# A list schedule in which all-SBUF VectorE instructions and GpSimd arithmetic take turns, with transfer leads and slacks set anew

## The chip, the cores and the metric

The kernel runs on one core of a Trainium2 chip. A time is device microseconds of one execution of the whole program. The core has five engines, each with its own queue that it works through in order: PE (matrix products, and transposes as products with an identity), DVE (VectorE), ACT (ScalarE), POOL (GpSimd) and SP, which here only issues transfers. SBUF holds the working tiles, PSUM takes what PE writes.

## The reference

One layer of an encoder serves 2048 prompt frames and 8 running streams of 16 new frames, with shared weights:

```
h = rms_norm(x, norm_g);  z = h @ w_in                       # (T,1024) @ (1024,3584)
u_a, v_a, g_a, q, k, v, g_b = split(z)
y_a = u_a * (tril(W_s) @ rms_norm(v_a) + b_s) * silu(g_a)    # per 128-position chunk, 4 heads
q, k = rms_norm(q), rms_norm(k)                              # two 64-wide halves per head
p1, p2 = softmax(q1 k1' / 8 - alibi), softmax(q2 k2' / 8 - alibi)   # block-causal, or past + new
y_b = rms_norm((p1 - lam * p2) @ v) * (1 - lam_init) * silu(g_b)
out = x + concat(y_a, y_b) @ w_out                           # also returned: new k, v and v_a rows
```

All tensors are float32. Most operands of PE are written as a sum of two rounded parts, high and low, so that one product becomes three (`mm3`) or two.

## The kernel before, in words

The program is first written down in one order and then sorted by a list scheduler, `Order`, once per build. What is written down:

- **Projection** (`stream`, `project`): 17 tiles of 128 frames (16 prompt tiles, one tile with all sample frames). `xload` scales a tile's rows on DVE (L552), `xpose` transposes it on PE (`x_tp`, L367) and `split` makes the high part with ACT (L428) and the low part with DVE (L429). `load_w` loads a block of the weights, makes the high part on ACT (L595) and the low part on DVE (L596). `project` gathers 3 products for each of 8 slices of 128 inputs, so 24 matmuls `acc` per tile and block. `vg_group` follows with squares, `rstd` on POOL (L435, L436), a scaling on DVE (`vn`, L693) and a split (`vhl`).
- **Sample attention** (`sample_scores`, `sample_values`), woven into the projection: cached keys are transposed (`sk_tp`), split into `skT` by ACT and DVE, multiplied (`sS`), completed by POOL (`slo`, L1074) and DVE (L1075); cached values are split by ACT and POOL (`sv`, L429 POOL), then multiplied (`sO`).
- **Prompt attention** (`attention`), in two stages: scores `S`, a running minimum on DVE (L858), exponentials on ACT (L862), the two softmaxes combined by DVE (`ex`, L874) or by ACT and POOL (L877, L878), transposed (`a_tp`), split into `aT`, multiplied with the values (`oT`), normalised (`o_tp`, L925 to L931).
- **Output** (`out_stream`): products `oo` with `w_out`, woven into the second attention stage, the sum with x on POOL (L1279) or DVE (L1281).

`constants` computes lambda from four loaded vectors (`keep1`, L415) by two DVE instructions (L417) near the start.

`Order` then fixes each engine's queue. `depend` finds which instruction needs which. `cost` gives each instruction a duration and a time after which its engine is free. `run` walks through time: the engine that can start earliest takes, of its instructions that are ready, the one that was written down first. An instruction's ready time is its latest producer's end plus a hop per engine plus a slack (L68: 350 ns for PE, 500 ns for SP; L69: `OTHER`, 150 ns for ACT, DVE and POOL). A transfer is taken to need `FETCH` = 3200 ns before its data begin to flow, one transfer after the other. The result is order alone: each engine works through its list, and the semaphores that the tile framework sets between engines stay the same in kind. Nothing on the chip waits for the planned times. In this plan DVE and POOL are independent of each other.

Of the kernel before, what the change touches and what calls it, by code (L numbers as in the profile page):

```python
# [18 lines left out]
PSUM = bass.MemoryType.PSUM  # L19
# [40 lines left out]
class Order:  # L60
# [4 lines left out]
    PE, ACT, DVE, POOL, SP = (mybir.EngineType.PE, mybir.EngineType.Activation, mybir.EngineType.DVE,  # L65
                              mybir.EngineType.Pool, mybir.EngineType.SP)

    SLACK = {PE: 350.0, SP: 500.0}  # L68
    OTHER, FETCH = 150.0, 3200.0  # L69

    class Node:
        def __init__(self, ins, idx):
# [45 lines left out]
    def depend(self):  # L118
        seen, last = {}, {}
        self.uses = {}  # L120
        for n in self.nodes:
            for ap, w in [(a, False) for a in n.reads] + [(a, True) for a in n.writes]:
                t = ap.bass_ap.tensor
                space = str(t.space)
                m, chip = self.region(ap, space), "DRAM" not in space
                lo = ap.bass_ap.offset
                box = lo, lo + sum(s * (k - 1) for s, k in ap.ap) + 1, chip and ap.ap[0][1] < P
                old = seen.setdefault(t.name, [])
                for m2, j, w2, box2 in old:
                    if (w or w2) and j != n.idx and (m & m2 or ((box[2] or box2[2]) and box[0] < box2[1] and  # L130
                                                                box2[0] < box[1])):
                        n.deps.add(j)
                if w and n.engine == self.PE:
                    if t.name in last:
                        n.deps.add(last[t.name])
                    last[t.name] = n.idx
                if w:
                    old[:] = [x for x in old if x[0] & ~m or x[1] == n.idx]
                old.append((m, n.idx, w, box))
                if chip and t.name not in n.tiles:  # L140
                    n.tiles.append(t.name)
                    self.uses.setdefault(t.name, []).append(n.idx)
# [45 lines left out]
    def cost(self, n):  # L188

        kind = type(n.ins).__name__[4:]  # L190
        size = max([math.prod([k for s, k in a.ap[1:]]) for a in n.reads + n.writes] or [1])
        accum = len(n.writes) > 1
        if n.dma:
            return 0.0, 560.0 if n.engine == self.POOL else 400.0
        if n.engine == self.PE:
            size = math.prod([k for s, k in n.writes[0].ap[1:]])
            t = 109.0 if size <= P else 4 + 0.4455 * size
            return t + 165, t
        if n.engine == self.ACT:
            t = 165 + 0.83 * size if kind == "TensorCopy" else 205 + 0.835 * size  # L200
            return (t + 180, t + 90) if accum else (t, t - 105)
        if n.engine == self.DVE:
            t = {"TensorTensor": 160 + 1.04 * size, "TensorReduce": 160 + 1.03 * size, "Memset": 100 + 0.5 * size,
                 "Reciprocal": 162.0}.get(kind, 205 + 1.04 * size)
            if kind == "TensorScalarPtr" and not n.ins.is_scalar_tensor_tensor:
                t = 170 + 0.56 * size
            return (t + 100, t - 40) if accum else (t, t - 85)
        if kind == "Memset":
            return 100 + 0.83 * size, 100 + 0.83 * size
        if "pow" in str(n.ins):  # L210
            return 300 + 200.0 * size, 250 + 200.0 * size
        t = 190 + 2.16 * size if kind == "TensorTensor" else 195 + 1.1 * size
        return t, t - 50

    def run(self):
        N = self.nodes
# [29 lines left out]
        left = {k: len(q) for k, q in self.queue.items()}  # L246
        users = {x: len(self.uses[x]) for x in self.tag}
        last, slot, taken, freed = {}, {}, set(), {}
        free = {n.engine: 0.0 for n in N}
        later, now_, held = {e: [] for e in free}, {e: [] for e in free}, set()  # L250
        out = {e: [] for e in free}
        dma = 0.0

# [18 lines left out]
        def arrive(i):  # L272
            if N[i].new:
                held.add(i)
            else:
                heapq.heappush(later[N[i].engine], (ready[i], i))

        def place():
            for i in sorted(held):
                got = buffer(i)  # L280
                if got:
                    for name, s in got[1]:
                        taken.add(s)
                        slot[name] = s
                        left[s[0]] -= 1
                    ready[i] = max(ready[i], got[0])
                    held.discard(i)
                    heapq.heappush(later[N[i].engine], (ready[i], i))
                    return True
            return False  # L290
# [3 lines left out]
                arrive(n.idx)  # L294
        while place():
            pass
        for _ in N:
            t, _, e = min((free[e] if now_[e] else max(free[e], later[e][0][0]), e.value if hasattr(e, "value") else str(e), e)
                          for e in free if now_[e] or later[e])
            while later[e] and later[e][0][0] <= t:  # L300
                heapq.heappush(now_[e], heapq.heappop(later[e])[1])
            i = heapq.heappop(now_[e])
            n = N[i]
            out[e].append(i)
            if n.dma:
                size = 4 * math.prod([k for s, k in n.writes[0].ap])
                dma = max(t + self.FETCH, dma) + max(size / 280, 60.0)
                end = dma + 200
            else:
                end = t + cost[i][0]  # L310
            free[e] = t + cost[i][1]
            for j in n.after:
                b = N[j].engine
                if b == e and not n.dma and not N[j].dma:
                    r = free[e]
                else:
                    r = end + reach.get(b, 35.0) + (self.SLACK.get(b, self.OTHER) if b != e or n.dma else 0)
                ready[j] = max(ready[j], r)
                N[j].wait -= 1
                if not N[j].wait:  # L320
                    arrive(j)
            more = list(first[i])
            for g in gate[i]:
                g[0] -= 1
                if not g[0]:
                    more += g[2]
            for j in more:
                ready[j] = max(ready[j], t)
                N[j].wait -= 1
                if not N[j].wait:  # L330
                    arrive(j)
            for name in n.tiles:
                if name in users:
                    last[name] = max(last.get(name, 0.0), end + 35)
                    users[name] -= 1
                    if not users[name]:
                        taken.discard(slot[name])
                        freed[slot[name]] = last[name]
            while held and place():
                pass  # L340
# [7 lines left out]
def trunk_step_kernel(  # L348
# [588 lines left out]
    def attention(sb, sl, groups, wmax, nk, nv, nex, comb, eng):  # L937
# [31 lines left out]
        for i, (key, j) in enumerate(units):  # L969
# [33 lines left out]
            for _, run in sorted(events, key=lambda e: e[0]):  # L1003
                yield run()
# [350 lines left out]
```

## Time and profile before

| | |
|---|---|
| median of 3 runs (lowest to highest) | 1421.57 us (1420.43 to 1421.87) |
| the profiled execution: time, span of its instructions | 1421.42 us, 1419.7 us |
| mean granted TensorE clock | 0.993 |
| busy: PE, DVE, ACT, POOL | 1364.3, 904.4, 789.6, 632.8 us |
| read from HBM, written | 130.86 MB, 42.47 MB |

The span runs from the program's first instruction to its last. Where a stretch is named below by two numbers, they are microseconds from the span's start. PE's matmuls overlap in their pipeline, so a busy PE is not PE at its peak; its idle time, and what ended each idle stretch, are listed by the view of waits.

### The profile page before, as it was taken

How to read it: one execution, taken by the hardware profiler on the slowest of the kernel's cores; microseconds unless marked ns; L12 is line 12 of the kernel's file. 1: busy time of each engine (PE TensorE's matmuls, PEld its weight loads, DVE VectorE, ACT ScalarE, POOL GpSimd, SP SyncE). 2: the span in 40 equal slices, each digit the busy share in tenths (PEclk: the TensorE clock that was granted, in tenths of full speed). 3: DMA queues.
4: the chain of work that ended last, by engine and by line, in shares of the span. 5: the costliest groups of instructions: out<-in, count | busy, mean ns of one | idle time of the engine just before them, and what ended most of it. 6: DMA issues, size and time to landing. Idle time of an engine off the chain costs nothing.

```text
span 1419.7 us, 27994 instructions
## 1 busy us (share of the span) xinstructions
PE 1364.3 (96%) x9892; PEld 1264.1 (89%) x9892; DVE 904.4 (64%) x2114; ACT 789.6 (56%) x1778; POOL 632.8 (45%) x796
## 2 busy tenths in 40 slices
PE   5999999999999999999999999998899999999998
PEld 5999999899998889999999999997788888888887
DVE  4432447766665684698987764324788897877722
ACT  4533336766565775566666454224677766676621
POOL 2251544656364564857435142022456545555400
PEclk9999999999999999999999999999899999999999
DMA  6533224554444475635443243245555534432323
GB/s 185 187 89 107 72 75 127 165 152 137 135 128 137 145 211 182 191 98 156 127 110 108 68 130 98 75 131 168 158 149 145 164 102 126 145 103 83 106 82 101
DMA packets 209245, 183.06 MB, mean 129 GB/s; under 512 B 21104, under 2 KB 167024, under 8 KB 209104
## 3 DMA queue, kind: packets, MB, share of 16 engines
q1 hardware_dynamic: 199280, 155.17, 37.0%
q0 software_dynamic: 9824, 26.09, 6.6%
q8 instruction: 78, 1.28, 0.4%
q14 instruction: 63, 0.52, 0.1%
HBM read 130.86 MB, written 42.47 MB: 122 GB/s over the span
## 4 chain that ended last, share of the span: by engine, by line
PE 71%; DVE 10%; ACT 6%; issue 5%; POOL 4%; DMA 3%; SPq 1%; DVEq 0%; POOLq 0%; ACTq 0%
PE acc L363 34%; PE oo L363 11%; PE S L363 7%; PE oT L363 6%; PE a_tp L367 4%; DVE ex L858 2%; DVE ex L874 2%; PE sS L363 2%; ACT ex L862 2%; DVE w L596 1%; PE sk_tp L367 1%; PE sO L363 1%; POOL sv L429 1%; PE y_tp L367 1%; DMA wraw<-in_w_in_dram 1%
## 5 line engine op out<-in xcount | busy, mean ns | idle before, releaser
L363 PE MATMUL acc<-w,xT 128*128 128x256 f32 x5376 | 723.6, 284 | 4.9 <-DVE w L596 2.0
L363 PEld LDWEIGHTS acc<-w,xT 128*128 128x128 f32 x5376 | 678.1, 190 | 17.9 <-DVE w L596 3.8
L363 PE MATMUL oo<-wo,yT 128*128 128x512 f32 x816 | 235.1, 402 | 1.5 <-ACT yT L428 1.2
L363 PE MATMUL S<-kT,qT 128*128 128x512 f32 (+3 forms) x688 | 186.0, 363 | 5.3 <-DVE sst L858 4.1
L862 ACT ACTIVATE ex<-ex,sst 128x128 f32<-128x128 f32 (+15 forms) x128 | 153.8, 1203 | 42.7 <-DVE sst L858 42.2
L596 DVE SCALAR_TENSOR_TENSOR w<-wraw,normg,w 128x256 fp32r<-128x256 f32 x224 | 120.1, 564 | 80.2 <-ACT w L595 73.3
L363 PEld LDWEIGHTS oo<-wo,yT 128*128 128x128 f32 x816 | 146.4, 188 | 26.9 <-ACT yT L428 2.0
L363 PE MATMUL oT<-aT,v 128*128 128x256 f32 x864 | 154.9, 295 | 0.0
L429 POOL TENSOR_TENSOR sv<-svraw,sv 128x512 fp32r<-128x512 f32 (+1 forms) x72 | 98.7, 1375 | 95.8 <-ACT sv L428 74.4
L858 DVE CUSTOM_DVE_ANT_0 ex<-S,dist,sst 128x512 f32<-128x512 f32 (+2 forms) x192 | 123.1, 652 | 27.4 <-PE S L363 25.5
L363 PEld LDWEIGHTS S<-kT,qT 128*128 128x128 f32 x688 | 112.1, 189 | 23.5 <-DVE sst L858 10.3
L363 PEld LDWEIGHTS oT<-aT,v 128*128 128x128 f32 x864 | 124.1, 192 | 5.1 <-DVE aT L429 0.3
L595 ACT ACTIVATE w<-wraw,normg 128x256 fp32r<-128x256 f32 x220 | 103.4, 504 | 43.6 <-PE acc L363 23.3
L428 ACT CAST aT<-a_tp 128x512 fp32r<-128x512 f32 (+1 forms) x144 | 79.8, 560 | 85.0 <-PE a_tp L367 78.2
L429 DVE TENSOR_TENSOR aT<-a_tp,aT 128x512 fp32r<-128x512 f32 (+1 forms) x144 | 93.9, 658 | 31.0 <-ACT aT L428 30.0
L367 PE MATMUL a_tp<-ident,ex 128*128 128x128 f32 x544 | 91.0, 279 | 8.5 <-DVE ex L874 5.4
L858 DVE CUSTOM_DVE_ANT_0 ex<-S,dist 128x512 f32<-128x512 f32 (+3 forms) x128 | 78.2, 628 | 17.0 <-PE S L363 14.0
L367 PEld LDWEIGHTS a_tp<-ident,ex 128*128 128x128 f32 x544 | 65.0, 142 | 25.7 <-issue 6.9
L1074 POOL TENSOR_TENSOR slo<-slo,dist_s 64x256 f32<-64x256 f32 (+1 forms) x64 | 50.7, 792 | 55.1 <-ACT slo L1073 52.2
L874 DVE SCALAR_TENSOR_TENSOR ex<-ex,sst 128x1024 f32<-128x1024 f32 (+4 forms) x64 | 68.8, 1094 | 1.7
L878 POOL TENSOR_TENSOR ex<-ex 128x1024 f32<-128x1024 f32 (+4 forms) x32 | 58.6, 1846 | 23.4 <-ACT ex L877 19.7
L429 POOL TENSOR_TENSOR v<-vraw,v 128x512 fp32r<-128x512 f32 x36 | 48.5, 1346 | 31.6 <-ACT v L428 31.4
(144 smaller groups left out, 1936.2 us busy)
## 6 DMA issues: line engine op xcount, KB each, us to landing
wraw<-in_w_in_dram SPq DMA_DIRECT2D x160, 128.0 KB, 2.7
skraw<-in_cache_k_dram SPq DMA_DIRECT2D x64, 256.0 KB, 3.2
svraw<-in_cache_v_dram SPq DMA_DIRECT2D x64, 256.0 KB, 3.1
kT<-k_scr POOLq DMA_DIRECT2D x20, 512.0 KB, 5.8
vraw<-out_dram SPq DMA_DIRECT2D x36, 256.0 KB, 3.1
y<-y_scr SPq DMA_DIRECT2D x34, 256.0 KB, 3.1
out_dram<-xo SPq DMA_DIRECT2D x34, 256.0 KB, 2.0
wraw<-in_w_in_dram SPq DMA_DIRECT2D x128, 64.0 KB, 2.4
```

The costliest lines, as they stand in the source:

```text
L363: pe.last = nc.tensor.matmul(*a, **k).ins
L367: pe.last = nc.tensor.transpose(*a, **k).ins
L428: act.copy(hi, src)
L429: (lo_eng or dve).tensor_tensor(out=lo, in0=src, in1=f(hi), op=ALU.subtract)
L595: act.activation(w[:, 0], r, AF.Copy, scale=normg[:, kc:kc + 1])
L596: dve.scalar_tensor_tensor(out=w[:, 1], in0=r, scalar=normg[:, kc:kc + 1], in1=f(w[:, 0]), op0=ALU.mult, op1=ALU.subtract)
L858: dve.tensor_tensor_reduce(out=ex[c][:, a:b], in0=s, in1=dist[:, off + a:off + b], scale=SLOPES[h], scalar=prev[c], op0=ALU.add, op1=ALU.m ...
L862: act.activation(ex[c][:, :w], ex[c][:, :w], AF.Exp, bias=prev[c], scale=-1.0, accum_out=st[:, c, 6:7])
L874: dve.scalar_tensor_tensor(out=p0, in0=p1, scalar=st[:, 1, 7:8], in1=p0, op0=ALU.mult, op1=ALU.add)
L878: pool.tensor_tensor(out=p0, in0=p1, in1=p0, op=ALU.add)
L1074: pool.tensor_tensor(out=lo, in0=lo, in1=dist_s[rh, x:x + w_], op=ALU.add)
```

## The change

Six edits, all in `Order` (line numbers below it grow by 31, so L429 becomes L460):

- `port` sorts instructions: POOL arithmetic is kind 2; a DVE instruction that reads two wide operands from SBUF, or a large single one in one form, is kind 1; all others, those with a PSUM operand above all, are kind 0.
- In `run`, ready instructions of kind 1 or 2 wait in a heap of their own, `turn`, and are taken only when the plan's other holder (`busy[2]` for DVE, `busy[1]` for POOL) is through; until then the engine takes other ready work.
- PE's slack falls from 350 to 180 ns, SP's from 500 to 300, `OTHER` from 150 to 50.
- `FETCH` falls from 3200 to 2300 ns.
- Two readers of one PSUM tile now count as ordered in `depend`.
- The costs of one-element DVE instructions and of ACT's sums are set anew; of two engines that can start at the same time, the first in a fixed list goes.

```diff
-    SLACK = {PE: 350.0, SP: 500.0}
-    OTHER, FETCH = 150.0, 3200.0
+    SLACK = {PE: 180.0, SP: 300.0}
+    OTHER, FETCH = 50.0, 2300.0
...
-                    if (w or w2) and j != n.idx and (m & m2 or ...
+                    if (w or w2 or "PSUM" in space) and j != n.idx and (m & m2 or ...
...
+    def port(self, n):
+        if n.dma or type(n.ins).__name__ == "InstMemset" or n.engine not in (self.DVE, self.POOL):
+            return 0
+        if n.engine == self.POOL:
+            return 2
+        wide = [a for a in n.reads if math.prod([k for s, k in a.ap[1:]]) > 8 and
+                "PSUM" not in str(a.bass_ap.tensor.space)]
+        psum = any("PSUM" in str(a.bass_ap.tensor.space) for a in n.reads + n.writes)
+        large = math.prod([k for s, k in n.writes[0].ap[1:]]) >= 512 and type(n.ins).__name__ == "InstTensorScalarPtr"
+        return int(len(wide) > 1 or (len(wide) == 1 and large and not psum))
...
+            lock = busy[2 if e == self.DVE else 1]
+            if turn[e] and lock <= t and (not now_[e] or turn[e][0] < now_[e][0]):
+                i = heapq.heappop(turn[e])
+            elif now_[e]:
+                i = heapq.heappop(now_[e])
+            else:
+                continue
...
             free[e] = t + cost[i][1]
+            if port[i]:
+                busy[port[i]] = free[e]
```

What stands where, at three places. **At the start**, on DVE: `x_240` is the fourth tile of x, `xT_225` and `xT_248` the low parts of the third and fourth, `keep1` holds the lambda vectors. Before:

```order
L596 SCALAR_TENSOR_TENSOR w_589<-wraw_587,normg_119,w_589 128x256
L429 TENSOR_TENSOR xT_225<-x_tp_226,xT_225 128x512
L412 TENSOR_SCALAR subg_102<-subg_102 128x128
L417 ISA keep1_669,lame_673<-keep1_669 128x64
L417 ISA lame_673 128x1
L417 ISA keep1_669,lame_673<-keep1_669 128x64
L417 ISA lame_673 128x1
L429 TENSOR_TENSOR xT_225<-x_tp_233,xT_225 128x512
L552 TENSOR_SCALAR x_240<-x_240,xst_243 128x1024
```

After, the same stretch of DVE's queue:

```order
L460 TENSOR_TENSOR xT_225<-x_tp_226,xT_225 128x512
L443 TENSOR_SCALAR subg_102<-subg_102 128x128
L460 TENSOR_TENSOR xT_225<-x_tp_233,xT_225 128x512
L583 TENSOR_SCALAR x_240<-x_240,xst_243 128x1024
L627 SCALAR_TENSOR_TENSOR w_589<-wraw_587,normg_119,w_589 128x256
L627 SCALAR_TENSOR_TENSOR w_594<-wraw_592,normg_119,w_594 128x256
L448 ISA keep1_669,lame_673<-keep1_669 128x64
L448 ISA lame_673 128x1
L448 ISA keep1_669,lame_673<-keep1_669 128x64
L448 ISA lame_673 128x1
L460 TENSOR_TENSOR xT_248<-x_tp_249,xT_248 128x512
L460 TENSOR_TENSOR xT_248<-x_tp_256,xT_248 128x512
```

The two lambda instructions went behind the third tile's second low part and the fourth tile's scaling; the fourth tile's low parts stand directly behind them. On PE, the first rows are the transposes of tiles and their products; eight transposes make one tile. Before:

```order
L367 MATMUL x_tp<-ident,x 128x128 x8
L363 MATMUL acc<-w,xT 128x256 x15
L367 MATMUL x_tp<-ident,x 128x128 x8
L363 MATMUL acc<-w,xT 128x256 x7
L367 MATMUL x_tp<-ident,x 128x128 x4
L363 MATMUL acc<-w,xT 128x256 x3
L367 MATMUL x_tp<-ident,x 128x128 x4
L363 MATMUL acc<-w,xT 128x256 x30
L367 MATMUL x_tp<-ident,x 128x128 x8
L363 MATMUL acc<-w,xT 128x256 x41
```

After, PE's first rows again:

```order
L398 MATMUL x_tp<-ident,x 128x128 x8
L394 MATMUL acc<-w,xT 128x256 x15
L398 MATMUL x_tp<-ident,x 128x128 x8
L394 MATMUL acc<-w,xT 128x256
L398 MATMUL x_tp<-ident,x 128x128 x4
L394 MATMUL acc<-w,xT 128x256 x10
L398 MATMUL x_tp<-ident,x 128x128 x4
L394 MATMUL acc<-w,xT 128x256 x22
L398 MATMUL x_tp<-ident,x 128x128 x8
L394 MATMUL acc<-w,xT 128x256 x48
```

Up to the fourth tile's transposes PE had 55 products and has 48. On SP's queue the last of the four lambda loads now stands behind one more load of x (512 KB) and two loads of `bias_s`.

**In the sample attention**, on DVE, around `skT_6674`, the low part of a pair of cached key blocks, for which PE's next key transposes wait. Before:

```order
L1075 ISA sst2_6599 64x1
L429 TENSOR_TENSOR saT_6738<-sa_tp_6739,saT_6738 128x4x64
L552 TENSOR_SCALAR x_6549<-x_6549,xst_6552 128x1024
L693 SCALAR_TENSOR_TENSOR vn_6485<-va_6690,vst_6697,sgug_121 128x128 x2
L429 TENSOR_TENSOR skT_6674<-sk_tp_6675,skT_6674 128x2x256
```

After, at the same place in DVE's queue:

```order
L1106 ISA sst2_6599 64x1
L460 TENSOR_TENSOR skT_6674<-sk_tp_6675,skT_6674 128x2x256
L460 TENSOR_TENSOR saT_6738<-sa_tp_6739,saT_6738 128x4x64
L583 TENSOR_SCALAR x_6549<-x_6549,xst_6552 128x1024
L460 TENSOR_TENSOR skT_6759<-sk_tp_6760,skT_6759 128x2x256
L460 TENSOR_TENSOR saT_6738<-sa_tp_6790,saT_6738 128x4x64
L583 TENSOR_SCALAR x_6638<-x_6638,xst_6641 128x1024
L460 TENSOR_TENSOR xT_6646<-x_tp_6647,xT_6646 128x512
L724 SCALAR_TENSOR_TENSOR vn_6485<-va_6690,vst_6697,sgug_121 128x128
```

`vn` and the scaling of x, which read only SBUF, went behind instructions that read PSUM. It is not so everywhere: at an earlier key block, `skT_3315`, the new order puts an all-SBUF instruction (`sa`, 96x1040) ahead that stood behind.

**In the second attention stage**, on DVE, around the combination of two softmaxes `ex_13817` (1280 columns, in pieces of 1024 and 256). Before:

```order
L867 TENSOR_SCALAR sst_13816<-sst_13816,neglam_103 128x1
L874 SCALAR_TENSOR_TENSOR ex_13817<-ex_13818,sst_13816,ex_13817 128x1024
L874 SCALAR_TENSOR_TENSOR ex_13817<-ex_13818,sst_13816,ex_13817 128x256
L858 ISA ex_13936,sst_13935<-S_13949,dist_13219,sst_13935 128x512
L858 ISA sst_13935 128x1
L858 ISA ex_13937,sst_13935<-S_13956,dist_13219,sst_13935 128x512
```

After, from the first piece to the second:

```order
L905 SCALAR_TENSOR_TENSOR ex_13817<-ex_13818,sst_13816,ex_13817 128x1024
L889 ISA ex_13937,sst_13935<-S_13956,dist_13219,sst_13935 128x512
L889 ISA sst_13935 128x1
L463 SCALAR_TENSOR_TENSOR qT_13976<-q_tp_13973,qT_13976 64x256
L962 SCALAR_TENSOR_TENSOR gbt_13723<-o_tp_13922,ost_13923,gbt_13723 128x128 x2
L889 ISA ex_13936,sst_13935<-S_13985,dist_13219,sst_13935 128x384
L889 ISA sst_13935 128x1
L460 TENSOR_TENSOR aT_13968<-a_tp_13963,aT_13968 128x512
L463 SCALAR_TENSOR_TENSOR qT_13976<-q_tp_13973,qT_13976 64x256
L889 ISA ex_13937,sst_13935<-S_14019,dist_13219,sst_13935 128x384
L889 ISA sst_13935 128x1
L905 SCALAR_TENSOR_TENSOR ex_13817<-ex_13818,sst_13816,ex_13817 128x256
```

Between the two pieces stand now ten rows that read PSUM; before there was none.

More of the change, by code (lines that the diff above doesn't have):

```diff
@@ L129, in depend @@
                 for m2, j, w2, box2 in old:
-                    if (w or w2) and j != n.idx and (m & m2 or ((box[2] or box2[2]) and box[0] < box2[1] and
+                    if (w or w2 or "PSUM" in space) and j != n.idx and (m & m2 or ((box[2] or box2[2]) and box[0] < box2[1] and
                                                                 box2[0] < box[1])):
@@ L200, in cost @@
             t = 165 + 0.83 * size if kind == "TensorCopy" else 205 + 0.835 * size
-            return (t + 180, t + 90) if accum else (t, t - 105)
+            return (t + 190, t + 90) if accum else (t, t - 105)
         if n.engine == self.DVE:
@@ L204, in cost @@
                  "Reciprocal": 162.0}.get(kind, 205 + 1.04 * size)
+            if size == 1:
+                return (270.0, 190.0) if kind == "TensorScalarPtr" else (165.0, 90.0)
             if kind == "TensorScalarPtr" and not n.ins.is_scalar_tensor_tensor:
@@ L248, in run @@
         last, slot, taken, freed = {}, {}, set(), {}
-        free = {n.engine: 0.0 for n in N}
-        later, now_, held = {e: [] for e in free}, {e: [] for e in free}, set()
+        free = {e: 0.0 for e in (self.POOL, self.DVE, self.ACT, self.PE, self.SP)}
+        later, now_, turn, held = {e: [] for e in free}, {e: [] for e in free}, {e: [] for e in free}, set()
+        port, busy = [self.port(n) for n in N], [0.0, 0.0, 0.0]
         out = {e: [] for e in free}
@@ L296, in run @@
             pass
-        for _ in N:
-            t, _, e = min((free[e] if now_[e] else max(free[e], later[e][0][0]), e.value if hasattr(e, "value") else str(e), e)
-                          for e in free if now_[e] or later[e])
-            while later[e] and later[e][0][0] <= t:
-                heapq.heappush(now_[e], heapq.heappop(later[e])[1])
-            i = heapq.heappop(now_[e])
+        left_over = len(N)
+        while left_over:
+            t, e = None, None
+            for x in free:
+                lock = busy[2 if x == self.DVE else 1]
+                for y in ((free[x],) if now_[x] else ()) + ((max(free[x], lock),) if turn[x] else ()) + (
+                        (max(free[x], later[x][0][0]),) if later[x] else ()):
+                    if t is None or y < t:
+                        t, e = y, x
+            while later[e] and later[e][0][0] <= t:
+                i = heapq.heappop(later[e])[1]
+                heapq.heappush((turn if port[i] else now_)[e], i)
+            lock = busy[2 if e == self.DVE else 1]
[5 more added lines that the diff above has]
+                continue
+            left_over -= 1
             n = N[i]
```

## The prediction

> **What bounds the kernel now.** First the page: busy times and the chain that ended last.
>
> ```profile
> span 1419.7 us, 27994 instructions
> PE 1364.3 (96%) x9892; PEld 1264.1 (89%) x9892; DVE 904.4 (64%) x2114; ACT 789.6 (56%) x1778; POOL 632.8 (45%) x796
> PE 71%; DVE 10%; ACT 6%; issue 5%; POOL 4%; DMA 3%; SPq 1%; DVEq 0%; POOLq 0%; ACTq 0%
> ```
>
> PE is the bound: 96% busy and 71% of the chain. The change leaves its 9892 matmuls as they are, so it can only win from PE's idle time, 1419.7 − 1364.3 = 55.4 us, and from waits that lie inside the busy time. Second, busy time by stretch, cut where the stages change. The columns are the stretch, its length, busy us (instructions) of PE, weight loads, DVE, ACT and POOL, then granted clock, DMA share and GB/s; the last row is the end alone.
>
> ```profile
> 0.00:60.00 60.00, 43.53 (x311) 41.03 (x312) 27.89 (x85) 27.88 (x54) 12.10 (x29) 0.94 0.61 188
> 60.00:230.00 170.00, 169.34 (x1429) 168.90 (x1428) 70.44 (x134) 64.51 (x148) 71.51 (x75) 1.00 0.34 98
> 230.00:560.00 330.00, 315.58 (x2462) 298.32 (x2461) 217.27 (x484) 213.94 (x517) 175.78 (x199) 1.00 0.51 153
> 560.00:900.00 340.00, 334.16 (x2654) 322.75 (x2653) 252.65 (x608) 198.84 (x537) 162.23 (x241) 1.00 0.44 120
> 900.00:1046.00 146.00, 136.86 (x910) 124.04 (x909) 72.33 (x177) 63.65 (x135) 49.16 (x65) 0.96 0.42 128
> 1046.00:1419.70 373.70, 364.83 (x2138) 309.11 (x2136) 263.86 (x630) 220.75 (x392) 162.04 (x188) 1.00 0.40 120
> 1415.90:1419.70 3.80, 0.00 (x0) 0.00 (x0) 0.69 (x1) 0.00 (x0) 0.00 (x0) 0.78 0.18 69
> ```
>
> PE is idle for 16.5 us in the first 60, 0.7 us while only the projection runs, 14.4 us in the sample attention, 5.8, 9.1 and 8.9 us in the three stretches of prompt attention; 3.8 of the last is the drain at the end (last row). Third, whom PE waited for: us in total, times, longest.
>
> ```profile
> PE x_tp L367 <- DVE x L552: 14.7, 2, 8.5
> PE a_tp L367 <- DVE ex L874: 5.4, 5, 2.3
> PE S L363 <- DVE sst L858: 4.1, 8, 1.1
> PE sk_tp L367 <- DVE skT L429: 3.3, 3, 1.6
> ...
> PE sS L363 <- DVE sst L1075: 0.2, 1, 0.2
> ```
>
> The opening wait of 8.5 us stays. Most of the rest is waiting for DVE. The rows below the first, the two dozen of the view counted whole, add up to 59 waits; most are under 1 us.
>
> Fourth, why a DVE that is 64% busy is late. Two groups of one size (128x128) and one form, then the weights' low parts (busy, mean ns) with their shortest and median duration, and POOL's values with theirs:
>
> ```profile
> L693 DVE SCALAR_TENSOR_TENSOR vn<-va,vst,sgug 128x128 f32<-128x128 f32 x68 | 35.9, 565 | 24.4 <-POOL vst L436 24.0
> L931 DVE SCALAR_TENSOR_TENSOR gbt<-o_tp,ost,gbt 128x128 f32<-128x128 f32 x64 | 19.5, 343 | 4.5 <-POOL ost L928 4.4
> L596 DVE SCALAR_TENSOR_TENSOR w<-wraw,normg,w 128x256 fp32r<-128x256 f32 x224 | 120.1, 564 | 80.2 <-ACT w L595 73.3 <-POOL w L592 5.8
> L596 DVE SCALAR_TENSOR_TENSOR w<-wraw,normg,w x224: 469/482/1886, 6.4 to 938.5; 128x256 fp32r<-128x256 f32 x112
> L429 POOL TENSOR_TENSOR sv<-svraw,sv x72: 1267/1294/2536, 64.6 to 576.3; 128x512 fp32r<-128x512 f32 x64, 16x512 fp32r<-16x512 f32 x8
> ```
>
> `gbt` has an operand in PSUM and takes 343 ns; `vn` reads SBUF alone and takes 565 on average. `w` takes 469 at best, 564 on average, up to 1886. POOL's `sv` goes from 1267 up to 2536. The lengthening on these two DVE rows is 68 × 0.22 + 224 × 0.095 = 36 us. Fifth, such a place in time, the longest `skT` wait (start, us, what):
>
> ```profile
> 500.39 1.27 POOL L429 TENSOR_TENSOR sv<-svraw,sv 128x512 fp32r<-128x512 f32 x1
> 500.46 1.62 DVE L693 SCALAR_TENSOR_TENSOR vn<-va,vst,sgug 128x128 f32<-128x128 f32 x2 [0.87 <-POOL vst L436]
> 502.00 0.68 DVE L429 TENSOR_TENSOR skT<-sk_tp,skT 128x512 fp32r<-128x512 f32 x1
> 502.74 0.66 PE L367 MATMUL sk_tp<-ident,skraw 128*128 128x128 f32 x4 [1.57 <-DVE skT L429]
> ```
>
> POOL starts 0.07 us ahead of DVE. DVE's two `vn` take 1.62 us where two times 0.34 (the `gbt` row) would do, and end with POOL's `sv` plus one `vn`. `skT`, next in DVE's queue, reads PSUM and could have run; PE stands 1.57 us for it. That is an all-SBUF DVE instruction and a POOL instruction excluding each other, and PE paying for what stands behind.
>
> **The change part by part.** The sum is made against the profiled execution, 1421.42 us, 0.15 below the median of 1421.57.
>
> *Start.* These rows of the timeline carry the fourth tile's wait; the last is of the transfers issued in the first 60 us (count, size of one, median us from issue to landing):
>
> ```profile
> 19.06 3.78 PE L363 MATMUL acc<-w,xT 128*128 128x256 f32 x30
> 27.33 0.23 DVE L417 CUSTOM_DVE_ANT_0 keep<-keep 128x64 f32<-128x64 f32 x1 [3.71 <-DMA keep<-in_lambda_k_dram]
> 28.09 0.74 DVE L552 TENSOR_SCALAR x<-x,xst 128x1024 f32<-128x1024 f32 x1
> 28.98 1.94 PE L367 MATMUL x_tp<-ident,x 128*128 128x128 f32 x8 [6.14 <-DVE x L552]
> x<-in_x_prompt_dram SPq DMA_DIRECT2D x9, 512.0 KB, 6.1
> ```
>
> DVE stands at the lambda instruction until its vectors land (27.3), with the fourth tile's scaling behind it, and PE idles 6.14 us. After the change the scaling goes first, but the tile's low parts stand behind lambda. So PE can run, ahead of the wait, the fourth tile's 8 transposes and all 3 × 24 = 72 products of three tiles in place of 55: 17 × 3.78/30 = 2.1 us, and half of 1.94 (it ran at half clock, below) = 1.0 us. Against that the last lambda vector is loaded behind one more x load; I take 1 us of delay. Sum −2. Ends: −6.1 if lambda lands early, +1 if that load (6.1 us, the last row) shifts it by 4.
>
> *Turns.* Instructions that wait for the other engine in the plan go behind those with a PSUM operand. At `skT_6674` both `vn` now stand behind `skT`: the 1.57 us go, and next due is ACT's half of `skT`. In the second attention stage:
>
> ```profile
> 1036.32 1.29 POOL L429 TENSOR_TENSOR v<-vraw,v 128x512 fp32r<-128x512 f32 x1 [2.21 <-ACT v L428]
> 1036.93 3.18 DVE L874 SCALAR_TENSOR_TENSOR ex<-ex,sst 128x1024 f32<-128x1024 f32 x2
> 1037.56 2.26 POOL L1279 TENSOR_TENSOR xo<-yo,xo 128x512 f32<-128x512 f32 x1
> 1040.83 0.62 PE L363 MATMUL S<-kT,qT 128*128 128x384 f32 x2 [1.14 <-DVE sst L858]
> L1090 DVE SCALAR_TENSOR_TENSOR sa<-sp,sst,sa x8: 1296/1296/1299, 239.8 to 535.8; 96x1040 f32<-96x1040 f32 x8
> ```
>
> Unhindered, the two pieces need about 1.30 (the last row, its median at 1040 elements) + 0.47 (shortest `w`, 256) = 1.8 us and took 3.18; PE's 1.14 us are less than that difference. Now ten rows with PSUM operands stand between the pieces, so S's bank comes free earlier. So at both places PE's whole wait hangs on the exclusion, but not all waits do, and a row such as `sa` before `skT_3315` gives some back. I take half of the idle time in the sample attention, −8 with the short waits inside busy PE (between 0 and −14.4); a third of it in the prompt stretches, 5.8, 9.1 and 8.9 us, so −2, −3 and −2 (the last without the drain at the end). A gain is not excluded anywhere, nor a loss: a `vn` put off delays its own split.
>
> [...]
>
> *Leads and slacks.* PE's margin is 0.17 us shorter, that of DVE and ACT 0.10 each. Each of the 59 late waits that stays would end up to 0.17 later: 59 × 0.17 = 10 us at most; with half of them gone, +4. Below nothing is possible too, as less slack lets every engine take useful work sooner. `FETCH` at 2300 is covered by distance:
>
> ```profile
> kT<-k_scr POOLq DMA_DIRECT2D x20, 512.0 KB, 5.8
> svraw<-in_cache_v_dram SPq DMA_DIRECT2D x64, 256.0 KB, 3.1
> skraw<-in_cache_k_dram SPq DMA_DIRECT2D x64, 256.0 KB, 3.2
> ```
>
> The plan's 2300 + 256 KB/280 + 200 ns = 3.4 us for `svraw` still exceeds the measured 3.1. For `kT` it gives 4.4 against 5.8, but no row of PE's waits names a transfer: the earlier tile's S, running until the buffer turns, hides it. If that cover were gone, 20 × 0.9 us = 18. I take 0. PSUM readers in order and the new small costs only correct the plan; 0.
>
> *Clock.* After the waits around 994 the clock fell:
>
> ```profile
> 995.00:1000.00 5.00, 3.57 (x18) 3.20 (x17) 2.46 (x5) 3.14 (x6) 3.16 (x5) 0.50 0.47 113
> ```
>
> PE worked 3.57 us at half clock, so about 1.8 us were lost. I leave that loss in the sum. [...]
>
> Sum: −2 − 8 − 2 − 3 − 2 + 4 = −13, so 1421.4 − 13 = 1408. A measurement here can tell about 0.2% (2.8 us) from no change.
>
> **The rivals.** *Chains too tight (slower).* In the sample attention a key block goes PE, ACT, DVE, PE, and the plan now leaves 0.10 + 0.10 + 0.17 = 0.37 us less for it. There are 64 such blocks (x64 in the row of `skraw`, 8 for each stream). If each comes late by all of it, 64 × 0.37 = 24 us; with the gains of the other stretches (−2 −2 −3 −2) the time is 1421 + 24 − 9 = 1436. It outweighs the rest from about 17/0.37 = 46 late chains. For it: DVE is 66% and ACT 65% busy there, so small delays meet. Against: 0.7 us of idle time in 60 to 230, where the same slack is not needed. Chance 0.15, at 1426 to 1436.
>
> *The turns don't hold on the chip.* At 500.39 POOL led by 0.07 us, and the margins that are left are of that order: drift swaps who goes first and waits are exchanged, not removed. Then the start's −2 and the slack's +4 remain: 1419 to 1424. Against: order alone puts PSUM readers ahead whatever the time. Chance 0.14.
>
> *Nearly all goes.* If the exclusion is behind four fifths of the idle time from 230 on (14.4 + 5.8 + 9.1 + 5.1, the last without 3.8 at the end, = 34.4), the lambda wait goes and the clock holds: 1421.4 − 27.5 − 6.1 − 1.8 = 1386. For it: both places looked at. Against: tighter slack. Chance 0.13, at 1386 to 1397.
>
> **How the numbers follow.** The forecast, 1398 to 1418, has 0.58. The range 1391 to 1425 takes in the second rival and part of the third, about 0.8. Faster by over 0.2% means under 1418.7: 0.58 + 0.13 + 0.04 of the second rival = 0.75. Within 0.2%: 0.09, the rest of it. Slower: 0.16, the first rival with an edge of the second.
>
> **What would show it.** Right: the mean of L693 (L724 after) falls towards 343 ns and that of `w` towards 469; PE's idle time in 230 to 560 falls to about 8 us; the largest `skT` wait shrinks; the start's second wait falls from 6.1 to about 4. Wrong: `vn` and `w` keep their means; or they fall, and PE's waits for `sk_tp`, `sS` and `aT` grow in number past 59; or lambda lands so late that the wait at the start is longer than 6.1 us.

## The result, and the profile after

The changed kernel takes 1397.18 us (median of 4 runs, 1394.42 to 1400.32), the kernel before 1421.0 (4 runs, 1419.94 to 1421.87): a ratio of 0.9833, 95% interval 0.9811 to 0.9856, or 23.8 us less. 1408 was predicted, within 1391 to 1425. The sign and the place were right; the gain is nearly twice the 13 us of the sum, and the time lies 0.8 us below the stretch that was held likeliest, 1398 to 1418. The profiled execution has a span of 1395.0 us. Its page, span and busy times:

```profile
span 1395.0 us, 27945 instructions
PE 1355.2 (97%) x9892; PEld 1258.4 (90%) x9892; DVE 889.4 (64%) x2114; ACT 794.0 (57%) x1778; POOL 615.9 (44%) x796
```

PE's idle time fell from 55.4 to 1395.0 − 1355.2 = 39.8 us, by 15.6; PE's busy time fell by 9.1 for the same 9892 matmuls. DVE is 15.0 us less busy and POOL 16.9, with as many instructions as before. Busy time by stretch, cut as before (length, busy us of PE, weight loads, DVE, ACT, POOL, granted clock, DMA share, GB/s):

```profile
0.00:60.00 60.00, 46.43 (x340) 43.33 (x341) 30.90 (x91) 30.19 (x60) 11.19 (x29) 0.97 0.66 197
60.00:230.00 170.00, 167.96 (x1422) 166.88 (x1420) 71.68 (x144) 69.74 (x150) 72.68 (x75) 1.00 0.36 101
230.00:560.00 330.00, 322.80 (x2526) 306.82 (x2525) 213.20 (x474) 215.21 (x518) 183.65 (x211) 1.00 0.54 155
560.00:900.00 340.00, 336.08 (x2707) 327.85 (x2707) 247.21 (x614) 198.12 (x534) 144.35 (x230) 1.00 0.43 118
900.00:1046.00 146.00, 139.29 (x902) 123.32 (x902) 86.37 (x215) 77.59 (x160) 61.10 (x82) 0.99 0.50 151
1046.00:1395.00 349.00, 342.68 (x2006) 290.18 (x2004) 240.04 (x579) 203.17 (x358) 142.95 (x172) 1.00 0.39 117
```

PE's idle time, length less busy, is now 13.6, 2.0, 7.2, 3.9, 6.7 and 6.3 us, where it was 16.5, 0.7, 14.4, 5.8, 9.1 and 8.9. The same cut holds slightly more work now (4288 matmuls up to 560 for 4202), so these are rough to a few us, but the pattern is that of the forecast: half of the sample attention's idle time is gone, and a quarter to a third in the three stretches behind it. Whom PE waited for, the five largest rows and three further down (total us, times, longest):

```profile
PE x_tp L398 <- DVE x L583: 8.7, 2, 8.3
PE a_tp L398 <- DVE ex L905: 4.1, 3, 1.8
PE acc L394 <- DVE w L627: 3.1, 3, 1.7
PE sO L394 <- ACT sv L459: 3.0, 5, 1.2
PE acc L394 <- ACT w L626: 1.8, 1, 1.8
...
PE S L394 <- DMA qT<-qT: 0.9, 2, 0.6
...
PE S L394 <- DVE sst L889: 0.6, 2, 0.4
...
PE sk_tp L398 <- DMA skraw<-in_cache_k_dram: 0.5, 1, 0.5
```

The wait of S for `sst` fell from 4.1 to 0.6, and the row in which `sk_tp` waited 3.3 us for `skT` is gone: these are the two steps looked at in detail. In their place stand waits for transfers (`qT`, `skraw` and two more, 2.7 us in all), of which there were none before, and longer ones for ACT's part of `w`. All rows of the view together are 40 waits and 35.0 us, for 61 and 50.0 before.

**The start.** On PE and on DVE:

```profile
14.96 1.07 PE L398 MATMUL x_tp<-ident,x 128*128 128x128 f32 x8 [0.37 <-DVE x L583]
17.82 0.39 PE L394 MATMUL acc<-w,xT 128*128 128x256 f32 x1 [1.79 <-ACT w L626]
...
24.93 1.03 PE L398 MATMUL x_tp<-ident,x 128*128 128x128 f32 x8
25.73 6.28 PE L394 MATMUL acc<-w,xT 128*128 128x256 f32 x48
```
```profile
27.33 0.23 DVE L448 CUSTOM_DVE_ANT_0 keep<-keep 128x64 f32<-128x64 f32 x1 [2.21 <-DMA keep<-in_lambda_k_dram]
```

The last lambda vector is used at 27.33, to the hundredth as before; the load of x ahead of it cost nothing. But DVE stands before it for 2.21 us in place of 3.71, and PE, which stood 6.14 us here, has the fourth tile's transposes and 48 products to do meanwhile. It pays earlier, 1.79 us for ACT's part of `w`. After 60 us PE has done 340 matmuls for 311.

**The second attention stage.** DVE's two pieces of `ex_13817`, and POOL beside them:

```profile
1016.97 1.28 DVE L905 SCALAR_TENSOR_TENSOR ex<-ex,sst 128x1024 f32<-128x1024 f32 x1
1017.52 0.94 POOL L958 TENSOR_TENSOR ost<-ost,sst 128x1 f32<-128x1 f32 x2 [3.04 <-ACT os L956]
...
1019.24 1.28 POOL L460 TENSOR_TENSOR v<-vraw,v 128x512 fp32r<-128x512 f32 x1
...
1020.48 1.29 POOL L1310 TENSOR_TENSOR xo<-yo,xo 128x512 f32<-128x512 f32 x1
...
1022.19 0.48 DVE L905 SCALAR_TENSOR_TENSOR ex<-ex,sst 128x256 f32<-128x256 f32 x1
```

The pieces take 1.28 and 0.48 us, together 1.76 where they took 3.18: the 1.30 + 0.47 that the unhindered rows gave. POOL's `v` and `xo`, which held them before, now run between them in 1.28 and 1.29 us (1.29 and 2.26 before), beside DVE's readers of PSUM. Only the tiny `ost` (two of one element, 0.94 us together) started in the shadow of the first piece. It is not so everywhere; the groups of DVE (busy us, mean ns):

```profile
L627 DVE SCALAR_TENSOR_TENSOR w<-wraw,normg,w 128x256 fp32r<-128x256 f32 x224 | 119.3, 559 | 54.2 <-ACT w L626 52.9 <-POOL w L623 0.3
...
L905 DVE SCALAR_TENSOR_TENSOR ex<-ex,sst 128x1024 f32<-128x1024 f32 x24 | 32.7, 1367 | 0.6
L724 DVE SCALAR_TENSOR_TENSOR vn<-va,vst,sgug 128x128 f32<-128x128 f32 x68 | 32.2, 507 | 21.1 <-POOL vst L467 21.0
...
L665 DVE TENSOR_TENSOR z<-z,qst 128x512 f32<-128x512 f32 x32 | 25.1, 785 | 28.4 <-POOL qst L467 28.4
```

`vn` fell from 565 to 507 ns and not to 343, `w` from 564 to 559 and not to 469. So the exclusion is far from gone. Of the two markers that the prediction named, `vn` lost a quarter of its excess and `w` hardly any of it while the time went down, and the question for the experiments is which part of the change pays, and through what.

### The profile page after: what moved, and what is told of

It reads as the page before. It is cut to its first block, busy times and chain, and to the rows that moved or that the text cites. A ratio compares the mean times of both kernels' runs of the same rounds, so it can differ in the third digit from the quotient of the medians.

```text
span 1395.0 us, 27945 instructions
## 1 busy us (share of the span) xinstructions
PE 1355.2 (97%) x9892; PEld 1258.4 (90%) x9892; DVE 889.4 (64%) x2114; ACT 794.0 (57%) x1778; POOL 615.9 (44%) x796
## 3 DMA queue, kind: packets, MB, share of 16 engines
q8 instruction: 78, 1.28, 0.4%
## 5 line engine op out<-in xcount | busy, mean ns | idle before, releaser
L394 PE MATMUL acc<-w,xT 128*128 128x256 f32 x5376 | 715.2, 283 | 9.1 <-DVE w L627 3.1
L460 POOL TENSOR_TENSOR sv<-svraw,sv 128x512 fp32r<-128x512 f32 (+1 forms) x72 | 94.4, 1314 | 89.4 <-ACT sv L459 63.4
L460 DVE TENSOR_TENSOR aT<-a_tp,aT 128x512 fp32r<-128x512 f32 (+1 forms) x144 | 94.0, 658 | 23.1 <-ACT aT L459 22.2
L889 DVE CUSTOM_DVE_ANT_0 ex<-S,dist 128x512 f32<-128x512 f32 (+3 forms) x128 | 78.7, 629 | 21.0 <-PE S L394 14.8
L905 DVE SCALAR_TENSOR_TENSOR ex<-ex,sst 128x1024 f32<-128x1024 f32 (+4 forms) x64 | 63.6, 1000 | 1.3
L715 POOL TENSOR_TENSOR gb<-sg,subg 128x256 f32<-128x256 f32 (+1 forms) x36 | 26.6, 738 | 82.0 <-DVE sg L690 81.7
```

Of the source, the lines that this page charges most:

```text
L394: pe.last = nc.tensor.matmul(*a, **k).ins
L460: (lo_eng or dve).tensor_tensor(out=lo, in0=src, in1=f(hi), op=ALU.subtract)
L715: pool.tensor_tensor(out=gb[:, 2 * k:2 * k + m], in0=s, in1=subg.unsqueeze(1).broadcast_to([P, m, P]), op=ALU.mult)
L889: dve.tensor_tensor_reduce(out=ex[c][:, a:b], in0=s, in1=dist[:, off + a:off + b], scale=SLOPES[h], scalar=prev[c], op0=ALU.add, op1=ALU.m ...
L905: dve.scalar_tensor_tensor(out=p0, in0=p1, scalar=st[:, 1, 7:8], in1=p0, op0=ALU.mult, op1=ALU.add)
```

## The experiments

Theory A: the turns make the gain, new slacks cost a little, the rest is worth nothing. Theory B: the shorter slacks and leads make it, since the means of `w` and `vn` hardly moved. All are edits of the kernel after; each is timed beside the kernel before on the same chip (1419.8 to 1421.2 us there).

**no_turns**: every instruction of kind 0.

```diff
     def port(self, n):
 
+        return 0
```

> The kernel after (1397.2 us), with every instruction of kind 0, so that nothing takes turns; the new leads, slacks, costs and the order of PSUM readers stay. Theory A, the turns make the gain and the slacks cost about 4 us: 1421 + 4 - 2 (start) = 1423, that is 1415 to 1426. Theory B, the shorter slacks make the gain (the mean of the low parts of the weights hardly fell, 564 to 559 ns, so the turns removed little of the exclusion): 1395 to 1403. Half and half: 1408 to 1412.

Measured: 1421.75 us, ratio 1.0002 (0.9992 to 1.0013). The whole gain is gone: A.

**turns_old_leads**: the counterpart.

```diff
-    SLACK = {PE: 180.0, SP: 300.0}
-    OTHER, FETCH = 50.0, 2300.0
+    SLACK = {PE: 350.0, SP: 500.0}
+    OTHER, FETCH = 150.0, 3200.0
```

> The kernel after with the old slacks (350, 500, 150) and the old lead of 3200 ns; the turns, the new costs and the order of PSUM readers stay. Theory A, the turns make the gain: 1391 to 1400, with vn at about 507 ns as in the kernel after. Theory B, the slacks make it: 1412 to 1422. Half and half: 1405 to 1412.

Measured: 1395.45 us, ratio 0.9817 (0.9797 to 0.9838), the fastest of this study, though its interval overlaps that of the kernel after. The new slacks and leads are not needed for the gain. Theory B has fallen.

**rest_only**: both edits, so no turns and old slacks and leads.

> The kernel after without turns and with the old slacks and lead: only the order of PSUM readers, the new small costs and the fixed order of engines are left of the change. Both theories hold these for corrections of the plan that are worth nothing: 1418 to 1424. If it is under 1415, a part that I costed at nothing makes a good share of the gain; if it is over 1427, the order that comes out of small edits scatters by more than I took.

Measured: 1415.24 us, ratio 0.9958 (0.9943 to 0.9973), outside the 1418 to 1424 that both theories gave. About 6 us under the kernel before come from parts that were costed at nothing.

**costs_only**: `rest_only` and, further, without the order of PSUM readers.

```diff
-                    if (w or w2 or "PSUM" in space) and j != n.idx and (m & m2 or ...
+                    if (w or w2) and j != n.idx and (m & m2 or ...
```

> Only the new small costs and the fixed order of engines of the change: without turns, with the old slacks and lead, and without the order of PSUM readers. With that order it was 1415.2, and before 1421.2. If planning PSUM readers in order is worth the 6 us (the tile framework keeps them in order on the chip, and the old plan did not know it): 1420 to 1423. If the small costs make it: 1413 to 1417.

Measured: 1415.72 us, ratio 0.9961 (0.9946 to 0.9976), level with `rest_only`. The order of PSUM readers shows no worth of its own; the few us come with the small costs and the fixed order of engines. Whether these costs help, or the order that came out is a lucky one, this run doesn't tell.

**old_fetch**: `FETCH` at 3200 alone.

```diff
-    OTHER, FETCH = 50.0, 2300.0
+    OTHER, FETCH = 50.0, 3200.0
```

> The kernel after with the lead of a transfer at 3200 ns again. I costed the shorter lead at nothing: 1394 to 1400 if that holds. If the shorter lead made part of the gain (the plan takes work for ready sooner after its transfer), 1402 to 1410; if it costs (PE now waits for qT, qraw and skraw for 0.5 to 0.9 us each), 1390 to 1394.

Measured: 1407.72 us, ratio 0.9902 (0.9883 to 0.9921): 8 us above the range of the case in which the lead is worth nothing. By itself it would say that the shorter lead is worth 10 us; the next two speak against that.

**old_slack**: the old slacks with the new lead.

```diff
-    SLACK = {PE: 180.0, SP: 300.0}
-    OTHER, FETCH = 50.0, 2300.0
+    SLACK = {PE: 350.0, SP: 500.0}
+    OTHER, FETCH = 150.0, 2300.0
```

> The kernel after (turns, lead 2300 ns) with the old slacks (350, 500, 150). With turns, old slacks and the old lead gave 1395.5, new slacks and the old lead 1407.7, new and new 1397.2. If the shorter lead is worth 10 us by itself: 1385 to 1390. If lead and slack only shift which order comes out, so that the 10 us were an accident of one order: 1394 to 1402. If a shorter lead costs with long slacks: 1403 to 1412.

Measured: 1397.72 us, ratio 0.9835 (0.9817 to 0.9854). With the old slacks the shorter lead changes +2.3 us, with the new ones −10.5: no effect of one sign.

**pe175**: PE's slack at 175 for 180 ns.

```diff
-    SLACK = {PE: 180.0, SP: 300.0}
+    SLACK = {PE: 175.0, SP: 300.0}
```

> The kernel after with PE's slack at 175 in place of 180 ns: no mechanism tells the two apart, only the order that comes out differs. It measures how far the time moves by the accident of an order. If the order's accident is small: 1395 to 1399.5. If accidents of 5 us and more are usual, as the 10 us between two leads suggest: further off than 4 us, to either side, most likely up (1401 to 1408).

Measured: 1401.8 us, ratio 0.9866 (0.9849 to 0.9883). An edit without a mechanism behind it moves the time by 4.6 us, the runs of the two kernels not overlapping (1400.77 to 1402.43 against 1394.42 to 1400.32), though the intervals of their ratios meet at the edge.

**turns_mid**: slacks and lead half way.

```diff
-    SLACK = {PE: 180.0, SP: 300.0}
-    OTHER, FETCH = 50.0, 2300.0
+    SLACK = {PE: 265.0, SP: 400.0}
+    OTHER, FETCH = 100.0, 2750.0
```

> The kernel after with slacks and lead half way between old and new (265 and 400, 100, 2750 ns). With turns the time has been 1395.5, 1397.2, 1397.7, 1401.8 and 1407.7 for five settings. If the settings have no effect of their own with turns, this is another draw from these: 1395 to 1405. Above 1410 or below 1390: a setting matters after all.

Measured: 1399.32 us, ratio 0.9856 (0.9833 to 0.9879). One more draw from the same lot. The six settings with turns average 1399.9 us and spread over 12; the four kernels without (before, `no_turns`, `rest_only`, `costs_only`) average 1418.4 and spread over 6.5.

The last four ask how the turns work, all with the old slacks and lead, between 1395.5 with turns and 1415.2 without. Theory A1: by keeping the two engines apart in time. Theory A2: by letting DVE's readers of PSUM, for which PE waits, go ahead.

**psum_first**: A2 alone, without any regard to the other engine.

```diff
-            if turn[e] and lock <= t and (not now_[e] or turn[e][0] < now_[e][0]):
+            if turn[e] and not now_[e]:
...
-            if port[i]:
-                busy[port[i]] = free[e]
```

> The kernel with the old slacks and lead (with turns 1395.5 us, without 1415.2), in which an instruction of kind 1 or 2 never waits for the other engine, but goes only when its own engine has nothing else ready: DVE's readers of PSUM always go first, and nothing keeps the two engines apart in time. Theory A1, the turns work by keeping the two engines apart (the lengthening on DVE and POOL fell by about 25 us): the gain is lost, 1411 to 1425. Theory A2, they work by what stands behind the lengthened instruction (PE's producers go ahead of it): 1392 to 1400. Both by halves: 1402 to 1409. Above 1425: pushing the others behind everything starves their own readers.

Measured: 1411.82 us, ratio 0.9932 (0.9912 to 0.9952). Of the 19.8 us it keeps 3.4, which is within the spread: A1, with little for A2. This run also puts the all-SBUF instructions behind everything else; whether a milder precedence of PSUM readers would keep more is not shown. The busy times of `turns_old_leads`, of `rest_only` and of `psum_first`, from their pages:

```profile
PE 1355.7 (97%) x9892; PEld 1261.8 (91%) x9892; DVE 886.2 (64%) x2114; ACT 788.5 (57%) x1778; POOL 621.4 (45%) x796
```
```profile
PE 1363.2 (96%) x9892; PEld 1267.1 (90%) x9892; DVE 910.8 (64%) x2114; ACT 791.1 (56%) x1778; POOL 628.9 (44%) x796
```
```profile
PE 1364.7 (97%) x9892; PEld 1267.6 (90%) x9892; DVE 903.0 (64%) x2114; ACT 789.7 (56%) x1778; POOL 624.0 (44%) x796
```

The sum over all of DVE is a plainer marker than the single means: 886 with turns, 911 without, 903 when only the readers of PSUM go first, for the same 2114 instructions.

**dve_waits** and **pool_waits**: one side yields. The second edit is the first with the two values exchanged.

```diff
-                lock = busy[2 if x == self.DVE else 1]
+                lock = busy[2] if x == self.DVE else 0.0
...
-            lock = busy[2 if e == self.DVE else 1]
+            lock = busy[2] if e == self.DVE else 0.0
```

> The kernel with turns, old slacks and old lead (1395.5 us), in which only DVE's instructions of kind 1 wait for POOL in the plan, and POOL's wait for nobody. Without turns it was 1415.2. Theory A1 with a side: a DVE instruction that starts after POOL's is held for up to 1.3 us, a POOL instruction that starts after DVE's for some 0.3 to 0.5, so DVE's yielding carries most: 1394 to 1402, DVE busy about 885 us. If both sides are needed: 1404 to 1410. An order's accident moves it by 5 either way.

> The counterpart: only POOL's instructions wait for DVE's of kind 1, and DVE's wait for nobody. Theory A1 with a side: most of the gain is lost, 1407 to 1416, DVE busy 897 us and more. If POOL's yielding carries the gain (POOL has time to spare, 45% busy): 1394 to 1402.

Measured: `dve_waits` 1400.43 us, ratio 0.9863 (0.9849 to 0.9878); `pool_waits` 1414.9 us, ratio 0.9961 (0.9949 to 0.9973). DVE's yielding alone brings 14.8 of the 19.8 us, and the rest is within the spread; POOL's alone brings 0.3. Their busy times, `dve_waits` first:

```profile
PE 1355.9 (97%) x9892; PEld 1262.5 (90%) x9892; DVE 884.9 (63%) x2114; ACT 789.6 (56%) x1778; POOL 621.6 (44%) x796
```
```profile
PE 1361.5 (96%) x9892; PEld 1264.7 (89%) x9892; DVE 912.4 (65%) x2114; ACT 790.9 (56%) x1778; POOL 635.5 (45%) x796
```

The rows at 500.39 in the prediction show the costly order: POOL began 0.07 us ahead, and DVE's two `vn` took 1.62 us for some 0.68. Counted over the trace of the kernel before, `w` took up to 1886 ns where an instruction of POOL had begun ahead of it and overlapped it (95 of 224), and at most 486 where POOL began later (26) or not at all (103); for `vn` the medians are 827 (21 of 68), 352 (10, with 892 to 1457 in the three where POOL began within 43 ns) and 347 ns (37). The pair adds on which side it costs: what the plan must avoid here is a DVE instruction issued just behind one of POOL.

PE's waits close the chain. Added up over the rows of the view, those that DVE ended come to 37.2 us in `rest_only`, 34.8 in `pool_waits` and 31.7 in `psum_first`, but to 24.7 in `dve_waits` and 25.0 in `turns_old_leads`.

**turns_margin**: the plan holds the other engine 150 ns beyond the planned end.

```diff
-                busy[port[i]] = free[e]
+                busy[port[i]] = t + cost[i][0] + 150.0
```

> The kernel with turns, old slacks and old lead (1395.5 us), in which the plan holds the other engine until the instruction's planned end plus 150 ns, in place of the time its own engine is free, 50 to 85 ns before that end. In the kernel after many of DVE's two-operand instructions still meet one of POOL, since the chip drifts from the plan. If the drift is of the order of 0.1 to 0.2 us: fewer meet, DVE busy under 880 us, 1386 to 1393. If the drift is larger than such a margin, or the longer hold takes back what it saves: 1395 to 1403, DVE busy 883 to 889 as before.

Measured: 1400.59 us, ratio 0.9862 (0.9846 to 0.9879). No better, and within the lot's spread no worse. DVE is busy for more, 895.5 us, not less:

```profile
L627 DVE SCALAR_TENSOR_TENSOR w<-wraw,normg,w 128x256 fp32r<-128x256 f32 x224 | 126.4, 593 | 47.4 <-ACT w L626 46.2
```

`w` is at 593 ns here, worse than in any other kernel of the study. A likely reading is that the longer hold moves more of them to where POOL is met against the plan; no run shows it. A margin of 150 ns, at any rate, does not keep the two apart. No experiment made a version that clearly beats the kernel after.

## Why the prediction was right, and where its sizes were off

Along the way from before to after by single steps, in medians: small costs and fixed order of engines 1421.0 to 1415.7 (−5.3), order of PSUM readers to 1415.2 (−0.5), turns to 1395.5 (−19.8), slacks and lead to 1397.2 (+1.7). The terms that missed most, small costs and what lies inside PE's busy time, both missed to the fast side.

*Bound.* Right in the main: of the 24.7 us between the two profiled spans 15.6 were PE's idle time and 9.1 lay inside its busy time. The waits hang on DVE's exclusion with POOL: where DVE yields, PE's idle time is 37.6 to 42.5 us (`turns_old_leads`, `dve_waits`), and in `rest_only`, `costs_only` and `no_turns` it is still 52 to 54.

*Start, −2.* The mechanism was right, and the turns brought it. The first 60 us of `rest_only` and of `turns_old_leads` (PE's busy us and matmuls first):

```profile
0.00:60.00 60.00, 43.42 (x311) 40.57 (x312) 28.14 (x85) 27.96 (x54) 11.83 (x29) 0.94 0.61 188
```
```profile
0.00:60.00 60.00, 46.41 (x333) 44.11 (x334) 30.55 (x91) 30.05 (x60) 11.61 (x29) 0.94 0.64 198
```

22 matmuls more at 0.126 us (30 in 3.78 us) are 2.8 us. The delay of 1 us that I took for lambda didn't come; the new wait of 1.79 for `w` I had not seen.

*Turns, −15 with the start apart.* Right in place and kind, somewhat small: −19.8 with the start, so some −17. By idle time the whole change gave 7.2, 1.9, 2.4 and 2.6 in the stretches for 8, 2, 3 and 2; the turns alone, from `rest_only` to `turns_old_leads`, gave 5.6, 2.4, 0.7 and 2.3. That is 14.1 and 11.0 for the 15 of the sum. What failed is the limit to idle time: the sum had the short waits inside PE's busy time only within its −8, and 9.1 us went there, 7.5 (1363.2 to 1355.7) between the two kernels that differ in the turns alone. "I leave that loss in the sum", of the half clock around 994, was one part: with the other spells an estimated 2.4 us, worked out in the last section. Of the two half-clock windows there one stayed, at 1002.41. Most of the fall in busy time is in the projection's `acc` (715.2 us for 723.6), and not by the clock, since the half-clock windows held 2.92 us of `acc` after and 1.65 before; its cause is open.

*Slacks, +4.* The sign is open. Without turns the new slacks and lead cost 6.5 us (1415.24 to 1421.75), with turns 1.7, and 5 ns of slack alone moved the time by 4.6. The term should have been a spread of ±6 around a small loss.

*`FETCH`, 0.* Neither borne out nor refuted: it changed −10.5 us with the new slacks and +2.3 with the old, both within the spread of 12. That one order would move by 10 us, I had not allowed for.

*Small costs and PSUM readers, 0.* The first came with −5.3 (−4.1 against the 1419.8 of the kernel before on the same chip), the second with −0.5. This is the term that was most off. About a fifth of the gain came with a part that I dismissed in half a sentence; by cause or by luck of the order is open, as the kernels without turns spread over 6.5.

*The rivals.* Too-tight chains: not seen, the sample attention lost half its idle time. That turns don't hold on the chip: wrong as a whole, right in part, since `w` kept its mean; what did hold is seen in DVE's total, lower with turns by 13 us (902.2 in `no_turns` to 889.4) to 25. The argument against this rival, that order alone would put PSUM readers ahead whatever the time, is not borne out by `psum_first`, which does so and keeps 3.4 us. That nearly all goes: the time came to the edge of its 1386 to 1397, but not by its mechanism: 39.8 us of idle time remain, and the busy time, with the clock in it, and the small costs gave what the waits did not. No run shows that shorter waits make the clock hold, for which its sum has 1.8 us; one of the two half-clock windows there stayed.

## What to carry to other kernels

When two engines lengthen each other's instructions, as DVE and POOL did here (`w` from 469 up to 1886 ns, `sv` from 1267 up to 2536), look for the one that the bounding engine waits for, and plan its yielding: on DVE alone that gave 14.8 of 19.8 us, on POOL alone 0.3, although the plan was followed only roughly. DVE's instructions are here the shorter ones (469 ns for 1267 at their shortest, `w` and `sv`), and DVE had readers of PSUM to go on with while POOL's arithmetic was all of one kind; no run tells which of these matters. Judge it by the summed busy time of the engine that is held, not by the mean of one group. In the eight kernels in which DVE yields the sum is 884.6 to 895.5 us, in the six others 902.2 to 912.4, and the times part in the same way (1395.5 to 1407.7, 1411.8 to 1421.8); `w`'s mean does not part them (538 to 593 ns, 564 to 589). Within either set the sum does not rank the kernels. And before a difference of a few us between two orders out of a scheduler is explained, change a number that means nothing and see how far the time moves; here it was 5 us, and 12 over all settings with turns, so only the 20 us of the turns are a finding.

## What the runs showed of the hardware

The spells of half clock (0.50 granted) lasted 3.41 us or twice that in both profiles (after the change from 19.37 and 1002.41, before it from 25.40, 994.78 and 1022.09), and the two after the change began without an idle stretch of that length ahead of them. Windows after the change, cut where the granted clock changes and at the same distance elsewhere (columns as above):

```profile
15.96:19.37 3.41, 1.48 (x10) 1.22 (x10) 1.97 (x4) 1.60 (x4) 0.72 (x1) 1.00 0.89 255
19.37:22.79 3.42, 3.42 (x15) 3.08 (x15) 1.91 (x4) 2.36 (x6) 0.69 (x2) 0.50 0.44 128
...
999.00:1002.41 3.41, 1.95 (x15) 1.57 (x14) 3.35 (x8) 1.54 (x4) 0.00 (x0) 1.00 0.13 38
1002.41:1005.83 3.42, 3.42 (x14) 3.12 (x15) 2.53 (x7) 1.56 (x3) 1.41 (x3) 0.50 0.20 38
1005.83:1009.24 3.41, 3.41 (x28) 3.19 (x27) 2.58 (x7) 3.41 (x7) 0.87 (x1) 1.00 0.43 114
```
```profile
572.33:575.74 3.41, 1.71 (x15) 1.47 (x14) 2.88 (x9) 1.78 (x4) 2.36 (x3) 1.00 0.45 138
575.74:579.16 3.42, 3.42 (x31) 3.42 (x31) 3.33 (x9) 1.07 (x4) 2.33 (x3) 1.00 0.67 182
```

PE was busy for 1.48 and for 1.95 of 3.41 us in two windows, and the window behind each ran at half clock, with 15 and 14 matmuls where the full windows at clock 1.00 in these rows hold 28 and 31. The longest wait was 1.79 us in the first and 1.18 in the second. Behind a window with 1.71 us of work the clock stayed at 1.00, and behind one with 2.06, in the rows below, it fell to 0.50; so busy time, as the profile models it, does not decide alone. Before the change the profile shows four half-clock windows with work in them (the row at 1018.67 stands ahead of the last):

```profile
28.81:32.22 3.41, 3.24 (x16) 3.27 (x17) 1.51 (x6) 2.53 (x6) 0.74 (x2) 0.50 0.64 165
...
994.78:998.19 3.41, 1.98 (x11) 1.61 (x9) 1.49 (x4) 2.04 (x4) 2.72 (x3) 0.50 0.46 126
998.19:1001.61 3.42, 3.42 (x18) 3.42 (x17) 1.55 (x3) 2.03 (x4) 1.84 (x3) 0.50 0.74 184
...
1018.67:1022.09 3.42, 2.06 (x14) 1.40 (x13) 3.36 (x6) 1.11 (x3) 0.39 (x1) 1.00 0.38 112
1022.09:1025.50 3.41, 3.04 (x12) 2.79 (x13) 2.95 (x9) 1.61 (x3) 0.84 (x2) 0.50 0.01 3
```

Taken as half of PE's busy time in them, the loss is an estimated (3.24 + 1.98 + 3.42 + 3.04)/2 = 5.8 us before, (3.42 + 3.42)/2 = 3.4 after, the 2.4 us above. It is that of one execution each: in the four of the kernel after the mean clock went from 0.993 to 0.998. The first matmuls are not in it. They took nearly twice as long in both kernels (eight transposes 1.97 us at 8.51 before and at 8.33 after, for 1.07 at 14.96 after), although the view shows a clock of 1.00 from 8 to 12 us in both. What sets the half clock off, no run shows: PE still worked for 1.48 and 1.95 us in the windows ahead. If a few short waits in one window bring it on, they can cost more than their own length: the window at 999.00 held 1.46 us of idle time, and the next lost an estimated 1.7 us, half of its 3.42, at half clock.
